# Layer 1's q, k and z projections computed with the weights as the stationary operand

## The chip, the cores and the metric

The kernel runs on one core of one Trainium2 chip. The metric is the device time of one execution in microseconds; of several runs the median is given. Five engines work side by side, each through its own queue in a fixed order: TensorE (PE, with its weight loads shown apart as PEld), VectorE (DVE), ScalarE (ACT), GpSimd (POOL) and SyncE (SP), which issues the transfers.

## What is computed

A decoder trunk of two layers over 256 tokens of width 2048. Layer 0 mixes by a gated spatial unit, layer 1 by causal attention with 16 heads of 128; with 256 tokens there is one key block, so every query sees its own block under the causal mask. Cut to layer 1, which the change touches:

```python
q, k, v, z = split(x @ w_in_b, 4)            # x 256 x 2048, each result 256 x 2048
for h in range(16):                           # heads of 128 columns
    s = q_h @ k_h.T * 128**-0.5               # 256 x 256
    s = where(key <= query, s, -inf)
    o_h = softmax(s) @ v_h
branch = o * silu(z)
y = branch @ w_out
x = layer_norm(ALPHA * x + y)
x = x + sigmoid(x @ w_gate) * (p @ w_proj)
```

All is float32 in, float32 out.

## The kernel before

**Products.** A float32 operand is split by `split` (line 71) or `load_weights` (line 110) into a high part that TensorE's fp32r format holds (a copy on ACT) and the rest (a subtraction on DVE). A product is then three matmuls: high by high, low by high, high by low. An operand's tile of 128 features is kept as `xs[k]`, 128 partitions by [high 256 tokens, low 256 tokens].

**Weights.** They stream through SBUF in chunks of 128 x 2048. `load_weights` fetches a chunk in two halves on SP's queue into `wr` (four buffers), makes `wh` on ACT (L121) and `wl` on DVE (L122); there are three buffers of each, and the loader runs two chunks ahead (`AHEAD`). The list `chunks` (lines 91 to 106) sets their order.

**Row units.** `row_unit` (line 182) takes one chunk: four of the 16 feature tiles, 512 output columns. The 128x128 piece of x is stationary, the 512 columns of weights move. For each k and each half m of the tokens it issues three matmuls of 512 columns, L204, L206 and L208, so 24 in a unit; `row_slice` calls four units for 512 output columns of all 256 tokens, and the result lies token-major in two PSUM banks.

**The order around the units.** At the end of each unit `tick` (line 158) calls what has come due in the list `later`; `at(n, f, ...)` puts a step there for the n-th unit end from now. The final order on each engine is set by the scheduler when the program is built.

**Attention before.** For every 512 columns q and k come by `row_slice` (lines 561 to 569) and are copied to SBUF by ACT (L567). `head` (line 501) turns one head's q and k by four PE transposes of 128x128 (L507, tile `tq`) and splits them; one unit later `scores` (L517 to L522, tile `sc`) forms the three causal 128x128 blocks, DVE and ACT make the probabilities, one unit later `probs` turns the three blocks (L542, tile `pt`) and splits them, and one unit later `values` (L555, tile `ov`) forms the head's output with the probabilities stationary:

```python
for m, bs in ((0, (0,)), (1, (1, 2))):
    steps = [(b, x, y) for b in bs for x, y in ((0, 0), (0, 1), (1, 0))]
    for a, (b, x, y) in enumerate(steps):
        nc.tensor.matmul(ov[:, m], p[:, x, b * P:(b + 1) * P], vk[b // 2][h // 4][:, y, hc], ...
```

That is nine matmuls of 128 columns. `gated` (line 348) then makes z by `row_slice`, multiplies silu(z) into `o` and turns the product by `turn` (L235, four transposes for 256 features) so that it can be the stationary operand of the output projection in `after` (line 381).

Of the kernel before, what the change touches and what calls it, by code (L numbers as in the profile page):

```python
# [10 lines left out]
AF = mybir.ActivationFunctionType  # L11
ALU = mybir.AluOpType

P = 128
D = 2048
S = 256
KT = D // P
NM = S // P
NS = D // 512
# [4 lines left out]
HD = 128  # L24
# [11 lines left out]
def f32(ap):  # L36
    return ap.bitcast(F32)
# [3 lines left out]
def decoder_trunk(ctx: ExitStack, tc: tile.TileContext, xT, pT, wv_a, wu_a, wz_a, w_sT, b_s,  # L41
# [5 lines left out]
    nc = tc.nc  # L47
# [7 lines left out]
    def t2(name):  # L55
        return act.tile([P, 512], F32, name=name, tag="t2", bufs=NT2)

    def t4(name):
        return act.tile([P, 1024], F32R, name=name, tag="t4", bufs=NT4)

    def r4(name):

        return act.tile([P, NM, 512], F32, name=name, tag="r4", bufs=NR4)

    def bank(name):
        return psum.tile([P, 512], F32, name=name, tag="bank", bufs=8)
# [4 lines left out]
    def split(src, n="s", g=2):  # L71

        t = t4(n).rearrange("p (g h s) -> p g h s", g=g, h=2)
        src = src.rearrange("p (g s) -> p g s", g=g)
        nc.scalar.activation(t[:, :, 0, :], src, AF.Copy)
        nc.vector.tensor_sub(t[:, :, 1, :], src, f32(t[:, :, 0, :]))
        return t
# [4 lines left out]
    def by_blocks(w):  # L82

        return [("p (b k c) -> p k b c", dict(b=4, k=4),
                 w[4 * n:4 * n + 4, :, 512 * c:512 * c + 512].rearrange("b p e -> p b e"))
                for n in range(NS) for c in range(4)]

    def flat(src):
        return [("", {}, src.rearrange("p (b e) -> p b e", b=4))]

    chunks = []
# [3 lines left out]
    for i in range(DEPTH):  # L95
        if i == 1:
            for h in range(2):
                for c in range(KT // 2):
                    chunks += flat(wv_b[h, c])
            q, k = by_blocks(wqkz_b[0:KT]), by_blocks(wqkz_b[KT:2 * KT])  # L100
            for n in range(NS):
                chunks += q[4 * n:4 * n + 4] + k[4 * n:4 * n + 4]
            chunks += by_blocks(wqkz_b[2 * KT:3 * KT])
        chunks += by_blocks(w_out[i])
        chunks += flat(w_proj[i, 0]) + flat(w_proj[i, 1])
        chunks += by_blocks(w_gate[i])
# [26 lines left out]
    ident = consts.tile([P, P], F32, name="ident")  # L133
# [20 lines left out]
    def at(units, f, *args):  # L154

        later.append([units, f, args])
# [25 lines left out]
    def row_unit(banks, ks, xs, order=None):  # L182


        NN = len(banks[0])
        pat, kw, wh, wl = weights()
        if pat:
            wh, wl = ([w.rearrange(pat, **kw)[:, i] for i in range(len(ks))] for w in (wh, wl))
            wh, wl = [[w] for w in wh], [[w] for w in wl]
        else:  # L190
            wh, wl = ([[w.rearrange("p (k n c) -> p k n c", k=len(ks), n=NN)[:, i, n] for n in range(NN)]
                       for i in range(len(ks))] for w in (wh, wl))

        def three(i, m, ns):
            k = ks[i]
            c = slice(m * P, (m + 1) * P)
            xh, xl = xs[k][:, 0, c], xs[k][:, 1, c]
            first, last = k == 0, k == KT - 1

            def o(n):  # L200
                return banks[m][n].rearrange("p (b c) -> p b c", b=4) if pat else banks[m][n]

            for n in ns:
                nc.tensor.matmul(o(n), xh, wh[i][n], start=first, stop=False)  # L204
            for n in ns:
                nc.tensor.matmul(o(n), xl, wh[i][n], start=False, stop=False)  # L206
            for n in ns:
                nc.tensor.matmul(o(n), xh, wl[i][n], start=False, stop=last)  # L208

        if order:  # L210
            for m, n in order:
                for i in range(len(ks)):
                    three(i, m, [n])
        else:
            for i in range(len(ks)):
                for m in range(NM):
                    three(i, m, range(NN))
        tick()
# [3 lines left out]
    def row_slice(xs, name="y"):  # L222

        banks = [[bank(name)] for _ in range(NM)]
        for c in range(4):
            row_unit(banks, range(4 * c, 4 * c + 4), xs, both if c == 3 else None)
        return [b[0] for b in banks]

    def turn(xs, j, rows, n="t"):

# [14 lines left out]
    xs = [None] * KT  # L245
# [96 lines left out]
    for n in range(NS):  # L342
        y = row_slice(xs, "u")
# [4 lines left out]
    def gated(o, xs):  # L348

        br = [None] * KT  # L350
        for n in range(NS):
            y = row_slice(xs, "z")
            for m in range(NM):
                t = t2("sz")
                nc.scalar.activation(t, y[m], AF.Silu)
                nc.vector.tensor_mul(o[n][:, m, :], o[n][:, m, :], t)
            for i in range(2):
                at(1 + i, turn, br, 2 * n + i, o, "b")
        return br
# [18 lines left out]
    br = gated(us, xs)  # L378
# [105 lines left out]
    xs = after(0, br)  # L484
# [3 lines left out]
    vk = [[None] * NS for _ in range(NM)]  # L488
# [8 lines left out]
    o = [None] * NS  # L497
    blocks = (slice(0, P), slice(P, 3 * P))
    w3 = slice(0, 3 * P)

    def head(h, q, k):

        c = slice((h % 4) * HD, (h % 4 + 1) * HD)
        tp = bank("tq")
        for j, r in enumerate((q, k)):
            for m in range(NM):
                nc.tensor.transpose(tp[:, j * S + m * P:j * S + (m + 1) * P], r[:, m, c], ident)  # L507
        at(1, scores, h, split(tp, "qk"))

    def scores(h, qk):  # L510
        qh, ql = qk[:, 0, 0, :], qk[:, 0, 1, :]
        kh, kl = qk[:, 1, 0, :], qk[:, 1, 1, :]
        c0, c1 = slice(0, P), slice(P, S)
        sc = bank("sc")

        t = sc.rearrange("p (a b) -> p a b", b=P)[:, 0:4:3, :]
        nc.tensor.matmul(t, qh[:, c0], qk[:, 1, :, c0], start=True, stop=False, skip_group_check=True)  # L517
        nc.tensor.matmul(sc[:, c0], ql[:, c0], kh[:, c0], start=False, stop=True, skip_group_check=True)
        t = sc[:, blocks[1]]
        nc.tensor.matmul(t, qh[:, c1], kh, start=True, stop=False, skip_group_check=True)  # L520
        nc.tensor.matmul(t, qh[:, c1], kl, start=False, stop=False, skip_group_check=True)
        nc.tensor.matmul(t, ql[:, c1], kh, start=False, stop=True, skip_group_check=True)  # L522
        s = t2("sm")
        nc.vector.tensor_add(s[:, w3], sc[:, w3], causal.rearrange("p a b -> p (a b)"))
        nc.vector.tensor_add(s[:, c0], s[:, c0], sc[:, 3 * P:4 * P])
        mx = small.tile([P, NM], F32, name="mx")
        sm = small.tile([P, NM], F32, name="sum")
        for m in range(NM):
            nc.vector.tensor_reduce(mx[:, m:m + 1], s[:, blocks[m]], axis=mybir.AxisListType.X, op=ALU.max)
        nc.vector.tensor_scalar(mx, mx, -QK_SCALE, None, op0=ALU.mult)  # L530
        for m in range(NM):
            nc.scalar.activation(s[:, blocks[m]], s[:, blocks[m]], AF.Exp, scale=QK_SCALE,
                                 bias=mx[:, m:m + 1], accum_out=sm[:, m:m + 1])
        nc.vector.reciprocal(sm, sm)
        for m in range(NM):
            nc.vector.tensor_scalar(s[:, blocks[m]], s[:, blocks[m]], sm[:, m:m + 1], None, op0=ALU.mult)
        at(1, probs, h, s)

    def probs(h, s):
        tp = bank("pt")  # L540
# [6 lines left out]
        at(1, values, h, p)  # L547

    def values(h, p):
        ov = bank("ov").rearrange("p (a c) -> p a c", c=P)  # L550
        hc = slice((h % 4) * HD, (h % 4 + 1) * HD)
        for m, bs in ((0, (0,)), (1, (1, 2))):
            steps = [(b, x, y) for b in bs for x, y in ((0, 0), (0, 1), (1, 0))]
            for a, (b, x, y) in enumerate(steps):
                nc.tensor.matmul(ov[:, m], p[:, x, b * P:(b + 1) * P], vk[b // 2][h // 4][:, y, hc],  # L555
                                 start=a == 0, stop=a == len(steps) - 1, skip_group_check=True)
        if h % 4 == 0:
            o[h // 4] = r4("o")
        nc.scalar.activation(o[h // 4][:, :, hc], ov[:, 0:NM], AF.Copy)

    for n in range(NS):
        rows = []
        for _ in range(2):
            y = row_slice(xs, "qk")
            rows.append(r4("qk"))
            for m in range(NM):
                nc.scalar.activation(rows[-1][:, m, :], y[m], AF.Copy)  # L567
        for h in range(4):
            at(1 + 2 * h, head, 4 * n + h, *rows)

    br = gated(o, xs)
    after(1, br)

# [54 lines left out]
```

## Time and profile before

| what | value |
|---|---|
| median of three runs | 1070.65 us (1070.04 to 1070.73) |
| the profiled execution | 1070.59 us |
| its span in the profile | 1068.9 us |
| mean granted TensorE clock | 0.999 of full speed |
| matmuls on PE | 4944 |
| moved over the span | 203.86 MB, 191 GB/s |

The profiled execution and the median agree to 0.1 us; 1.7 us of the execution lie outside the span. In the profile "busy" is the time in which an engine has at least one instruction under way. Matmuls are pipelined, and their recorded lengths overlap, so what one costs is read from the distance between the starts of two, in the view of instructions in order of time.

### The profile page before, as it was taken

To read this page: it belongs to the slowest core of one execution; us is meant where nothing else is said; L and a number is where in the kernel's file an instruction comes from. 1 tells how busy PE (TensorE), PEld (TensorE's weight loads), DVE (VectorE), ACT (ScalarE), POOL (GpSimd) and SP (SyncE) were. 2 spreads that over 40 slices of the span, in tenths; PEclk is the share of its full clock that TensorE was granted. 3 is DMA by queue.
4 is the path that set the end of the run, shared out by engine and by line. 5 is a ranking of instruction groups with operands and counts; after the bars stand their busy time and mean duration, and the time that the engine had idled before them with its cause. 6 is when DMAs were issued, how large, how long until landed. Compare 5 with 4: busy or idle time off the path is not lost.

```text
span 1068.9 us, 12836 instructions
## 1 busy us (share of the span) xinstructions
PE 1057.5 (99%) x4944; PEld 878.1 (82%) x4944; DVE 616.8 (58%) x763; ACT 499.5 (47%) x659; POOL 24.5 (2%) x46
## 2 busy tenths in 40 slices
PE   8999999999999999999999999999999999999997
PEld 6888888888888878888888888888888888887886
DVE  5646774555555695564545465555566555668552
ACT  5545453545433455444434455454465443345442
POOL 1100110000000000000000000000000000000000
PEclk9999999999999999999999999999999999999999
DMA  7775795566555555555555554444646455555561
GB/s 259 269 257 183 247 299 185 184 204 199 188 184 191 194 169 186 189 182 181 196 197 194 198 160 158 158 158 158 197 158 197 166 199 195 192 184 170 198 204 40
DMA packets 97262, 203.86 MB, mean 191 GB/s; under 512 B 6912, under 2 KB 9232, under 8 KB 97200
## 3 DMA queue, kind: packets, MB, share of 16 engines
q1 hardware_dynamic: 95184, 196.63, 54.9%
q0 software_dynamic: 2016, 6.40, 2.3%
q8 instruction: 39, 0.64, 0.3%
q14 instruction: 23, 0.19, 0.1%
HBM read 200.86 MB, written 2.15 MB: 190 GB/s over the span
## 4 chain that ended last, share of the span: by engine, by line
PE 82%; issue 14%; DMA 2%; DVE 1%; ACT 0%; POOL 0%; SPq 0%; POOLq 0%; ACTq 0%; DVEq 0%
PE qk L204 5%; PE g L208 5%; PE qk L208 5%; PE qk L206 5%; PE g L206 5%; PE g L204 5%; PE y L206 5%; PE y L204 5%; PE y L208 5%; PE z L204 4%; PE z L206 4%; PE z L208 4%; PE u L206 3%; PE u L204 3%; PE u L208 3%
## 5 line engine op out<-in xcount | busy, mean ns | idle before, releaser
L122 DVE TENSOR_TENSOR wl<-wr,wh 128x1024 fp32r<-128x1024 f32 (+1 forms) x366 | 433.4, 1204 | 334.0 <-ACT wh L121 324.7
L121 ACT ACTIVATE wh<-wr 128x1024 fp32r<-128x1024 f32 (+1 forms) x366 | 372.2, 1041 | 466.4 <-PE y L206 152.6
L204 PE MATMUL g<-wh,xn 128*128 128x512 f32 x256 | 101.7, 397 | 0.0
L204 PE MATMUL z<-wh,x 128*128 128x512 f32 x256 | 101.4, 396 | 0.0
L204 PE MATMUL qk<-wh,x 128*128 128x512 f32 x256 | 101.3, 396 | 0.0
L204 PE MATMUL y<-wh,b 128*128 128x512 f32 x256 | 100.1, 391 | 0.0
L208 PE MATMUL g<-wl,xn 128*128 128x512 f32 x256 | 100.0, 391 | 0.0
L208 PE MATMUL qk<-wl,x 128*128 128x512 f32 x256 | 100.0, 391 | 0.0
L208 PE MATMUL z<-wl,x 128*128 128x512 f32 x256 | 100.0, 390 | 0.0
L206 PE MATMUL qk<-wh,x 128*128 128x512 f32 x256 | 99.9, 390 | 0.0
L206 PE MATMUL z<-wh,x 128*128 128x512 f32 x256 | 99.8, 390 | 0.0
L206 PE MATMUL g<-wh,xn 128*128 128x512 f32 x256 | 99.8, 390 | 0.0
L208 PE MATMUL y<-wl,b 128*128 128x512 f32 x256 | 99.7, 389 | 0.0
L206 PE MATMUL y<-wh,b 128*128 128x512 f32 x256 | 99.6, 389 | 0.0
L208 PEld LDWEIGHTS z<-wl,x 128*128 128x128 f32 x256 | 48.1, 188 | 10.2
L208 PEld LDWEIGHTS g<-wl,xn 128*128 128x128 f32 x256 | 48.0, 188 | 10.2
L208 PEld LDWEIGHTS qk<-wl,x 128*128 128x128 f32 x256 | 48.1, 188 | 10.2
L208 PEld LDWEIGHTS y<-wl,b 128*128 128x128 f32 x256 | 48.1, 188 | 10.1
L204 PEld LDWEIGHTS y<-wh,b 128*128 128x128 f32 x256 | 48.1, 188 | 9.9
L206 PEld LDWEIGHTS y<-wh,b 128*128 128x128 f32 x256 | 48.1, 188 | 9.7
L206 PEld LDWEIGHTS g<-wh,xn 128*128 128x128 f32 x256 | 48.2, 188 | 9.5
L206 PEld LDWEIGHTS qk<-wh,x 128*128 128x128 f32 x256 | 48.1, 188 | 9.4
(142 smaller groups left out, 1421.9 us busy)
## 6 DMA issues: line engine op xcount, KB each, us to landing
wr<-in_wqkz_b SPq DMA_DIRECT2D x96, 512.0 KB, 4.1
wr<-in_w_out SPq DMA_DIRECT2D x64, 512.0 KB, 4.1
wr<-in_w_gate SPq DMA_DIRECT2D x64, 512.0 KB, 4.1
wr<-in_wu_a SPq DMA_DIRECT2D x32, 512.0 KB, 4.3
wr<-in_wz_a SPq DMA_DIRECT2D x32, 512.0 KB, 4.1
wr<-in_wv_b SPq DMA_DIRECT2D x32, 512.0 KB, 3.9
wr<-in_wv_a SPq DMA_DIRECT2D x26, 512.0 KB, 5.3
gb<-vecs POOLq DMA_DIRECT2D x24, 256.0 KB, 5.9
```

Of the source, the lines that this page charges most:

```text
L121: nc.scalar.activation(hi[:, c], raw, AF.Copy)
L122: nc.vector.tensor_sub(lo[:, c], raw, f32(hi[:, c]))
L204: nc.tensor.matmul(o(n), xh, wh[i][n], start=first, stop=False)
L206: nc.tensor.matmul(o(n), xl, wh[i][n], start=False, stop=False)
L208: nc.tensor.matmul(o(n), xh, wl[i][n], start=False, stop=last)
```

## The change

q, k and z of layer 1 are made feature-major: `column_unit` takes a chunk that holds one tile of 128 output features for all 16 feature tiles of x. The weight piece is stationary and x moves: one matmul of 512 columns multiplies the high weights by [high x, low x] at once, one of 256 columns multiplies the low weights by high x. The bank then holds two halves of 256 tokens, which `halves_sum` adds (a copy on ACT, an addition on DVE). The values are formed with v stationary and the probabilities moving, so the head's output is feature-major as well; the block of the later queries with the later keys needs one more addition. The transposes of q, k and of the gated branch go. The transposed probabilities are taken two units behind the scores instead of one. The chunks of these weights are fetched in another order and cut, with the same bytes.

```diff
-            q, k = by_blocks(wqkz_b[0:KT]), by_blocks(wqkz_b[KT:2 * KT])
-            for n in range(NS):
-                chunks += q[4 * n:4 * n + 4] + k[4 * n:4 * n + 4]
-            chunks += by_blocks(wqkz_b[2 * KT:3 * KT])
+            for h in range(KT):
+                chunks += flat(wqkz_b[h]) + flat(wqkz_b[KT + h])
+            for f in range(KT):
+                chunks += flat(wqkz_b[2 * KT + f])
...
+    def column_unit(xs, joined=False):
+        ps = bank("f")
+        wh, wl = (t.rearrange("p (k c) -> p k c", k=KT) for t in weights()[2:])
+        for k in range(KT):
+            feature_product(ps, wh[:, k, :], wl[:, k, :], xs, k, joined)
+        tick()
+        return ps
+
+    def feature_product(ps, wh, wl, xs, k, joined=False):
+        lh = (ps[:, 0:S], wl, xs[k][:, 0, :])
...
+            ms = [(ps, wh, xs[k].rearrange("p h s -> p (h s)"))]
+            ms.insert(k < KT - 1, lh)
+        for j, m in enumerate(ms):
+            nc.tensor.matmul(*m, start=k == 0 and j == 0, stop=k == KT - 1 and j == len(ms) - 1,
+                             skip_group_check=True)
+
+    def halves_sum(o, ps):
+        nc.scalar.activation(o, ps[:, 0:S], AF.Copy)
+        nc.vector.tensor_add(o, o, ps[:, S:2 * S])
...
-    def head(h, q, k):
-
-        c = slice((h % 4) * HD, (h % 4 + 1) * HD)
-        tp = bank("tq")
-        for j, r in enumerate((q, k)):
-            for m in range(NM):
-                nc.tensor.transpose(tp[:, j * S + m * P:j * S + (m + 1) * P], r[:, m, c], ident)
-        at(1, scores, h, split(tp, "qk"))
...
-        at(1, probs, h, s)
+        at(2, probs, h, s)
...
     def values(h, p):
...
+        steps = ((0, c0, 0, p[:, 0, c0]), (0, c0, 0, p[:, 1, c0]), (0, c0, 1, p[:, 0, c0]),
+                 (1, slice(P, 3 * P), 0, p[:, :, c1]), (1, slice(P, S), 1, p[:, 0, c1]))
+        for j, (m, n, a, b) in enumerate(steps):
+            nc.tensor.matmul(ov[:, n], vk[m][h // 4][:, a, hc], b, start=j == 0, stop=j == 4,
+                             skip_group_check=True)
...
+        nc.scalar.activation(t, ov[:, 0:S], AF.Copy)
+        nc.vector.tensor_add(t[:, P:S], t[:, P:S], ov[:, S:3 * P])
+
+    def head(h, t):
+        at(1, scores, h, split(t, "qk"))
...
+    for h in range(KT):
+        t = t2("qk")
+        for j in range(2):
+            halves_sum(t[:, j * S:(j + 1) * S], column_unit(xs))
+        head(h, t)
+
+    br = [None] * KT
+    for j in range(KT // 2):
+        t = t2("sz")
+        for u in range(2):
+            halves_sum(t[:, u * S:(u + 1) * S], column_unit(xs))
+        nc.scalar.activation(t, t, AF.Silu)
+        nc.vector.tensor_mul(t, t, o[j // 2][:, j % 2, :])
+        t = split(t, "b")
+        br[2 * j:2 * j + 2] = [t[:, u] for u in range(2)]
     after(1, br)
```

The change moves instructions, so their order on two engines follows, before and changed, over one head of the attention in its steady state. In the rows `x_3143` to `x_3673` are the eight pairs of x's feature tiles, `f` is the bank of a column unit, and a count behind a row stands for instructions alike in a row.

TensorE before: the end of a unit with the scores of one head and the values of the head before, and the start of the next unit.

```order
L208 MATMUL qk<-wl,x_3673 128x512
L517 MATMUL sc<-qk 128x2x128
L518 MATMUL sc<-qk 128x128
L520 MATMUL sc<-qk 128x256
L521 MATMUL sc<-qk 128x256
L522 MATMUL sc<-qk 128x256
L555 MATMUL ov<-vk,pb 128x128 x9
L204 MATMUL qk<-wh,x_3143 128x512
L206 MATMUL qk<-wh,x_3143 128x512
```

TensorE before, one unit later: the four transposes of the next head's q and k stand next to those of the probabilities.

```order
L208 MATMUL qk<-wl,x_3185 128x512
L507 MATMUL tq<-ident,qk 128x128 x4
L542 MATMUL pt<-ident,sm 128x128 x3
L204 MATMUL qk<-wh,x_3305 128x512
```

TensorE with the change: the end of a k unit, with the values of the head before.

```order
L247 MATMUL f<-x_3673,wh 128x512
L247 MATMUL f<-x_3673,wl 128x256 x2
L247 MATMUL f<-x_3673,wh 128x512
L573 MATMUL ov<-pb,vk 128x256 x4
L573 MATMUL ov<-pb,vk 128x128
L247 MATMUL f<-x_3143,wh 128x512
L247 MATMUL f<-x_3143,wl 128x256
L247 MATMUL f<-x_3143,wh 128x512
L247 MATMUL f<-x_3143,wl 128x256
```

The units alternate between 512 and 256 columns, the last two feature tiles with the two short ones side by side; the values are five matmuls. At the end of the q unit stand the three transposes of the probabilities and then the five matmuls of the scores, and no transposes of q and k:

```order
L247 MATMUL f<-x_3673,wh 128x512
L558 MATMUL pt<-ident,sm 128x128 x3
L533 MATMUL sc<-qk 128x2x128
L534 MATMUL sc<-qk 128x128
L536 MATMUL sc<-qk 128x256
L537 MATMUL sc<-qk 128x256
L538 MATMUL sc<-qk 128x256
L247 MATMUL f<-x_3143,wh 128x512
```

VectorE before, from one head's reciprocal of the sums to the next head's masked scores.

```order
L534 RECIPROCAL sum<-sum 128x2
L536 TENSOR_SCALAR sm<-sm,sum 128x128
L536 TENSOR_SCALAR sm<-sm,sum 128x256
L122 TENSOR_TENSOR wl<-wr,wh 128x1024
L76 TENSOR_TENSOR qk<-tq,qk 128x2x256
L546 TENSOR_TENSOR pb<-pt,pb 128x384
L122 TENSOR_TENSOR wl<-wr,wh 128x1024
L524 TENSOR_TENSOR sm<-sc,causal 128x384
L122 TENSOR_TENSOR wl<-wr,wh 128x1024
L525 TENSOR_TENSOR sm<-sm,sc 128x128
```

VectorE with the change, the same stretch.

```order
L550 RECIPROCAL sum<-sum 128x2
L552 TENSOR_SCALAR sm<-sm,sum 128x128
L552 TENSOR_SCALAR sm<-sm,sum 128x256
L252 TENSOR_TENSOR qk<-qk,f 128x256
L122 TENSOR_TENSOR wl<-wr,wh 128x1024
L579 TENSOR_TENSOR o<-o,ov 128x128
L76 TENSOR_TENSOR qk<-qk 128x2x256
L122 TENSOR_TENSOR wl<-wr,wh 128x1024 x2
L562 TENSOR_TENSOR pb<-pt,pb 128x384
L540 TENSOR_TENSOR sm<-sc,causal 128x384
L252 TENSOR_TENSOR qk<-qk,f 128x256
L541 TENSOR_TENSOR sm<-sm,sc 128x128
```

The additions of the halves (L252) stand in the queue, each behind the end of its unit on TensorE, and three of a head's four weight subtractions (L122) stand behind the second of them.

## Rows read from the trace of the kernel before

**Rows 1.** The page's busy times: us, share of the span, instructions.

```profile
PE 1057.5 (99%) x4944; PEld 878.1 (82%) x4944; DVE 616.8 (58%) x763; ACT 499.5 (47%) x659; POOL 24.5 (2%) x46
```

**Rows 2.** The page's chain that ended last, shares of the span by engine.

```profile
PE 82%; issue 14%; DMA 2%; DVE 1%; ACT 0%; POOL 0%; SPq 0%; POOLq 0%; ACTq 0%; DVEq 0%
```

**Rows 3.** Waits of PE: us in total, times, longest us.

```profile
PE pt L542 <- DVE sm L536: 0.5, 1, 0.5
```

**Rows 4.** Order of time, PE: first and last of an undisturbed run of 512-column matmuls (start us, length us).

```profile
589.67 0.39 PE L206 MATMUL qk<-wh,x 128*128 128x512 f32 x1
...
613.01 0.39 PE L208 MATMUL qk<-wl,x 128*128 128x512 f32 x1
```

**Rows 5.** Order of time, PE: turning one head's q and k.

```profile
613.25 0.60 PE L507 MATMUL tq<-ident,qk 128*128 128x128 f32 x4
613.60 0.48 PE L204 MATMUL qk<-wh,x 128*128 128x512 f32 x1
613.91 0.40 PE L206 MATMUL qk<-wh,x 128*128 128x512 f32 x1
```

**Rows 6.** Groups of instructions on PE by line, over the span: busy us, mean ns.

```profile
L507 PE MATMUL tq<-ident,qk 128*128 128x128 f32 x64 | 9.6, 272 | 0.0
...
L235 PE MATMUL tp<-ident,o 128*128 128x128 f32 x32 | 4.8, 272 | 0.0
```

**Rows 7.** Order of time, PE: one head's scores and another's values.

```profile
644.80 0.28 PE L517 MATMUL sc<-qk 128*128 128x256 f32 x1
644.91 0.22 PE L518 MATMUL sc<-qk 128*128 128x128 f32 x1
644.97 0.34 PE L520 MATMUL sc<-qk 128*128 128x256 f32 x1
645.14 0.28 PE L521 MATMUL sc<-qk 128*128 128x256 f32 x1
645.26 0.28 PE L522 MATMUL sc<-qk 128*128 128x256 f32 x1
645.38 1.11 PE L555 MATMUL ov<-vk,pb 128*128 128x128 f32 x9
...
646.62 0.40 PE L206 MATMUL qk<-wh,x 128*128 128x512 f32 x1
```

**Rows 8.** Order of time, PE: layer 0's spatial product, 256 columns each, and what follows.

```profile
134.32 0.88 PE L329 MATMUL sp<-vs,ws 128*128 128x256 f32 x6
135.03 0.40 PE L204 MATMUL u<-wh,x 128*128 128x512 f32 x1
...
135.50 0.39 PE L208 MATMUL u<-wl,x 128*128 128x512 f32 x1
...
136.19 0.39 PE L208 MATMUL u<-wl,x 128*128 128x512 f32 x1
```

**Rows 9.** Groups on PEld by line: busy us, mean ns.

```profile
L208 PEld LDWEIGHTS qk<-wl,x 128*128 128x128 f32 x256 | 48.1, 188 | 10.2
...
L329 PEld LDWEIGHTS sp<-vs,ws 128*128 128x128 f32 x48 | 6.8, 190 | 0.6
```

**Rows 10.** Busy times by stretch: four heads' rounds; us, then each engine's busy us and instructions.

```profile
631.49:684.72 53.23, 53.23 (x277) 45.25 (x276) 31.23 (x56) 26.61 (x48) 0.00 (x0) 1.00 0.49 161
```

**Rows 11.** Groups on DVE by line and shape: busy us, mean ns.

```profile
L76 DVE TENSOR_TENSOR qk<-tq,qk 128x512 fp32r<-128x512 f32 x16 | 10.9, 684 | 1.1 <-ACT qk L75 1.1
...
L76 DVE TENSOR_TENSOR x<-xr,x 128x512 fp32r<-128x512 f32 x7 | 5.2, 752 | 5.8 <-ACT x L75 5.8
...
L525 DVE TENSOR_TENSOR sm<-sm,sc 128x128 f32<-128x128 f32 x16 | 4.5, 282 | 0.1
...
L459 DVE TENSOR_TENSOR sg<-sg,pp 128x256 f32<-128x256 f32 x4 | 1.5, 422 | 12.8 <-ACT sg L458 12.8
```

**Rows 12.** The page's transfers by line: KB each, us to landing.

```profile
wr<-in_wqkz_b SPq DMA_DIRECT2D x96, 512.0 KB, 4.1
...
wr<-in_wv_b SPq DMA_DIRECT2D x32, 512.0 KB, 3.9
```

More of the change, by code (lines that the diff above doesn't have):

```diff
@@ L227, in row_slice @@
         return [b[0] for b in banks]
+    def column_unit(xs, joined=False):
[7 more added lines that the diff above has]
+        lh = (ps[:, 0:S], wl, xs[k][:, 0, :])
+        if joined:
+            ms = [(ps[:, 0:S], wh, xs[k][:, h, :]) for h in range(2)] + [lh]
+        else:
+            ms = [(ps, wh, xs[k].rearrange("p h s -> p (h s)"))]
[6 more added lines that the diff above has]
+        nc.vector.tensor_add(o, o, ps[:, S:2 * S])
     def turn(xs, j, rows, n="t"):
@@ L549, in values @@
     def values(h, p):
-        ov = bank("ov").rearrange("p (a c) -> p a c", c=P)
+        ov = bank("ov")
         hc = slice((h % 4) * HD, (h % 4 + 1) * HD)
[L552 to L556, printed above, removed]
+        c0, c1 = slice(0, S), slice(2 * P, 3 * P)
+        steps = ((0, c0, 0, p[:, 0, c0]), (0, c0, 0, p[:, 1, c0]), (0, c0, 1, p[:, 0, c0]),
[3 more added lines that the diff above has]
+                             skip_group_check=True)
         if h % 4 == 0:
             o[h // 4] = r4("o")
[L559 to L571, printed above, removed]
+        t = o[h // 4][:, (h % 4) // 2, (h % 2) * S:(h % 2 + 1) * S]
+        nc.scalar.activation(t, ov[:, 0:S], AF.Copy)
[16 more added lines that the diff above has]
+        br[2 * j:2 * j + 2] = [t[:, u] for u in range(2)]
     after(1, br)
```

## The prediction

> **What bounds the kernel now.** I read the page's busy times first [rows 1]: PE is busy for 1057.5 of 1068.9 us and no other compute engine for more than 58%. The chain that ended last is 82% PE and 14% unexplained issue time [rows 2]; DVE and ACT hold 1% of it. PE's own waits in the stage that changes come to 0.5 us, once, for a head's probabilities [rows 3]. So the end is set by how long PE needs to start one matmul after another, and a matmul's price is the distance between starts, not its recorded length (0.39 us, which overlaps its neighbour). In an undisturbed stretch 103 matmuls of 512 columns separate the starts at 589.67 and 613.01 [rows 4], 0.2266 us each. Short matmuls come in bursts between them, and every one of them delays the end, because PE has nothing to wait for that could swallow it.
>
> **What goes.**
>
> *Transposes of q and k, and of the gated branch.* From the first of four transposes to the second matmul behind them 0.66 us pass [rows 5]; one matmul of 512 would take 0.227, so a burst of four costs 0.433 us. There are 64 transposes of q and k and 32 of the branch [rows 6], 24 bursts: 24 x 0.433 = 10.4 us.
>
> *Values.* Nine matmuls of 128 columns and the long one behind them take 645.38 to 646.62, 1.24 us [rows 7]; less 0.227 that is 1.013 us a head. In their place come four of 256 and one of 128 columns. With 0.123 us for 256 columns (below) and 0.11 for the one of 128 (it and the 256 behind it span 644.91 to 645.14, 0.23, of which 0.12 belong to the latter [rows 7]) that is 0.60. Saved: 0.41 x 16 heads = 6.6 us.
>
> *The one wait for probabilities.* They are now due two units behind the scores, not one; the 0.5 us [rows 3] goes. What is late next there is the split of q and k, treated below.
>
> Together 10.4 + 6.6 + 0.5 = 17.5 us.
>
> **What is added on PE.** For one tile of 128 output features and one feature tile of x the old form spends six matmuls of 512 on four such tiles, 6 x 0.2266 / 4 = 0.340 us. The new form spends one of 512 and one of 256 columns. There are 48 x 16 = 768 such pairs, so a nanosecond on the pair is 0.77 us. No row shows 512 and 256 in turns; the nearest rows bound the pair:
>
> - Cheapest: the first 256-column matmul behind a long one takes 644.80 to 644.91, 0.11 us [rows 7]. The pair is then 0.337, and the units become 2.3 us shorter.
> - Nearest to it are 256-column matmuls that each have their own weights, as here. In a row they start 0.12 apart (645.14, 645.26, 645.38 [rows 7]; six in 0.71 us [rows 8]). But the long ones behind such a burst are slow for a while. From the first of six (134.32) to the end of five long ones (136.19) pass 1.87 us; less 5 x 0.2266 that is 0.74, or 0.123 us for each short one with its consequences [rows 8]. The pair is 0.350, and 768 of them cost 0.0097 x 768 = 7.5 us more than before.
> - Dearest: every long one is as slow as the two that follow a burst at once, 135.03 to 135.50, 0.235 each [rows 8]. The pair is 0.355 and the units cost 11.6 us more.
>
> I take the middle, 7.5, since it is the only one that holds the after-effect and spreads it over the short matmuls that caused it. By the Trainium skill, "TensorE: Matmul & The Clock Gate", section "Back-to-back issue gap", a gap is the columns over 2.4 plus 2.5 ns, that is 215.8 ns for 512 and 109.2 ns for 256; the pair would then cost 325.0 against 323.7 ns for the old share, an estimate of 1.0 us in all, and the sum would come to 1054.1. The trace shows 226.6 where that rule has 215.8, so I don't use it.
>
> **What is added beside PE, costed at nothing.** Four heads' rounds last 53.23 us with DVE busy for 31.23 [rows 10], 7.8 of 13.3 us a head. Added on DVE per head are two additions of 256 columns (0.42 each), one of 128 (0.28), and a split that reads SBUF instead of PSUM (0.752 against 0.684) [rows 11]: 1.2 us, so 9.0 us in a round that shrinks to about 12.7 (32 pairs of 0.350, 1.5 for scores, probabilities and values). ACT, busy for 26.61 of the 53.23 [rows 10], trades its copies of q and k for copies of half banks. The cover is PE: a weight chunk is split two units before it is used, and the split of q and k has the whole next unit (5.6 us) for two copies and two DVE steps. Should that cover go, PE waits for `wl` or for the scores' operands; that is the first rival.
>
> The additions wait for PE in DVE's queue, and three of four weight subtractions of a head stand behind the second. From the end of the q unit to that addition's end I count 7.6 us (its own unit's end at 0.3 + 0.6 + 5.6 = 6.5, the ACT copy and the addition 0.4 each, the hand-overs), then three subtractions, one addition and the split, 4.7 us: 12.3 of a round of 12.7. The chunk so finished is needed a unit later, so some 5 us remain.
>
> Transfers: the same bytes in 96 issues at the same place in SP's queue; the flat cut that they now have lands in 3.9 us where the old one took 4.1 [rows 12]. POOL's queue keeps its order. No price.
>
> **The sum.** 1070.6 (the profiled execution; the median of the runs is 0.1 higher) - 17.5 + 7.5 = **1060.6 us**. With the ends of the pair's price, 1050.8 and 1064.7.
>
> **Rivals.**
>
> *DVE's queue becomes the bound (slower).* Place: the additions of the halves, L252, in the rounds of the 16 heads. Each waits for PE's unit to end and for ACT's copy, with weight subtractions queued behind. It decides once DVE's busy 9.0 us and its in-order waits exceed the 12.7 us of a round, so with over 3.7 us of waits a head. From there every microsecond costs 16. With 4.8 us of waits it is 1.1 x 16 = 17.6 us on top: 1078. For it: DVE waits for ACT and PE several times in a round, and new waits come in. Against it: in the old rounds it had 5.5 us free of 13.3 and PE never waited for it but once [rows 3, 10]; loads run two chunks ahead. Chance 0.06.
>
> *Weight loads become the bound (slower).* The number of loads in these units rises from 1152 to 1536, and each is recorded at 188 ns [rows 9]. If a matmul could not start before the recorded end of its load, the pair would cost 2 x 0.188 = 0.376 and the units 27.6 us more: 1080.7. Against it: the spatial product's loads are recorded at 190 ns, each with its own matmul, and the matmuls start 0.12 apart all the same [rows 8, 9], so loads overlap. Chance 0.03. The Trainium skill, "Perfetto Trace Analysis", section "Identifying the Most-Contended Engine", judges TensorE by the busy share of its weight loads and not by matmul time; by that rule this is the resource that the change spends more of, and no row here shows long and short matmuls in turns.
>
> *The short matmul hides (faster still).* If each 256 costs 0.11 in the alternation and leaves no slow matmul behind it, the time is 1051 to 1054. For it is the first matmul of a burst; against it the after-effect. Chance 0.05.
>
> *In between.* A smaller wait in the attention's rounds, about 0.5 us a head, takes back 8 us: 1066 to 1072. Chance 0.05.
>
> **How the numbers follow.** The forecast has 0.81. Its range reaches from a pair of 0.341 to one of 0.355, with 1 us of small changes at the top: 1054 to 1066; outside lie the last case, the cheap one and the two slower ones. A measurement of this kernel tells 0.2%, 2.1 us, from no change. Faster by more: 0.81 + 0.05 + 0.02 = 0.88; within it, 0.03; slower, 0.09.
>
> **What would show it right or wrong.** Right: PE without a wait between the value projection and the output projection; in the column units starts 0.23 and 0.12 us apart; still two bursts a head, without the four transposes; the stage from the first q unit to the output projection 10 us shorter; all else as before. The pair's price is the step most likely to be off: the distance of two L247 matmuls of 512 columns, 0.350, gives it directly. A row "PE f <- DVE wl" or "PE sc <- DVE qk" among the waits would show the first rival; distances near 0.376 with PEld without gaps the second. A change in the time of layer 0, which is built the same, would make the comparison itself doubtful.

## The result and the profile after

The changed kernel takes 1058.1 us (median of four runs, 1057.6 to 1058.2) against 1070.7 of the kernel before on the same chip: a ratio of 0.988, 95% interval 0.987 to 0.990. Forecast were 1060.6 us, 10 us less than before; it is 12.6 us less. The profiled execution's span is 1056.3 us, before 1068.9.

The page's busy times, chain by engine and transfers of the changed kernel answer to [rows 1, 2, 12].

```profile
PE 1044.7 (99%) x5168; PEld 879.4 (83%) x5168; DVE 636.2 (60%) x827; ACT 499.0 (47%) x687; POOL 24.2 (2%) x46
...
issue 67%; PE 27%; DVE 3%; DMA 1%; ACT 1%; POOL 0%; SPq 0%; POOLq 0%; ACTq 0%; DVEq 0%
...
wr<-in_wqkz_b SPq DMA_DIRECT2D x96, 512.0 KB, 3.6
```

PE is still busy for 99% of the span. The chain now calls most of its time "issue", where it said PE before. That is no idle time, as the stretch from the first q unit to the output projection shows; why the view follows the chain another way is not known. The stretch is given for the kernel before first, then for the changed one (us; busy us of PE, PEld, DVE, ACT, POOL; clock).

```profile
564.28:868.12 303.84, 303.35 (x1513) 255.40 (x1512) 171.80 (x271) 153.86 (x245) 4.31 (x8) 1.00 0.53 173
```

```profile
564.43:856.49 292.06, 292.06 (x1745) 257.35 (x1744) 191.58 (x335) 153.21 (x272) 0.00 (x0) 1.00 0.52 174
```

This stage is 11.78 us shorter, PE is busy for all of it at the full clock, and DVE does 20 us more work in it. The output projection behind it, in which two of the gated branch's bursts of transposes stood, went from 88.0 to 87.05 us. Together that is 12.7 us. Every other stage from the end of layer 0's first projection on has kept its length to 0.1 us. That first projection varies from one execution to the next, so small differences between kernels are read below from the stage and not from the total.

One head's round in the changed kernel, TensorE in order of time (start us, length us): the values behind a k unit, and the probabilities and scores behind the next q unit.

```profile
650.09 0.69 PE L573 MATMUL ov<-pb,vk 128*128 128x256 f32 x5
650.62 0.45 PE L247 MATMUL f<-x,wh 128*128 128x512 f32 x1
650.91 0.28 PE L247 MATMUL f<-x,wl 128*128 128x256 f32 x1
651.02 0.40 PE L247 MATMUL f<-x,wh 128*128 128x512 f32 x1
651.26 0.28 PE L247 MATMUL f<-x,wl 128*128 128x256 f32 x1
...
655.18 0.40 PE L247 MATMUL f<-x,wh 128*128 128x512 f32 x1
...
656.23 0.49 PE L558 MATMUL pt<-ident,sm 128*128 128x128 f32 x3
656.47 0.37 PE L533 MATMUL sc<-qk 128*128 128x256 f32 x1
```

From 651.02 to 655.18 lie twelve pairs, 0.347 us each. The units of z, which have no bursts between them, are dearer: from one place in a unit to the same place two units on pass 11.30 us, 5.65 a unit and 0.353 a pair.

```profile
838.83 0.40 PE L247 MATMUL f<-x,wh 128*128 128x512 f32 x1
...
850.13 0.40 PE L247 MATMUL f<-x,wh 128*128 128x512 f32 x1
```

PE's recorded waits in the changed kernel are those at the start of the program and around the layer norms and the output; none lies in the column units, nor do those of its weight loads, and the one of [rows 3] is gone.

### The profile page after: what moved, and what is told of

The parts are those of the page before. It is cut to its first block, busy times and chain, and to the rows that moved or that the text cites. A ratio compares the mean times of both kernels' runs of the same rounds, so it can differ in the third digit from the quotient of the medians.

```text
span 1056.3 us, 13379 instructions
## 1 busy us (share of the span) xinstructions
PE 1044.7 (99%) x5168; PEld 879.4 (83%) x5168; DVE 636.2 (60%) x827; ACT 499.0 (47%) x687; POOL 24.2 (2%) x46
## 4 chain that ended last, share of the span: by engine, by line
issue 67%; PE 27%; DVE 3%; DMA 1%; ACT 1%; POOL 0%; SPq 0%; POOLq 0%; ACTq 0%; DVEq 0%
PE g L206 6%; PE g L208 6%; PE g L204 6%; PE v L206 2%; PE v L208 2%; PE v L204 2%; DVE wl L122 1%; PE tp L260 1%; DMA wr<-in_wv_a 1%; PE u L206 1%; PE u L204 1%; PE u L208 0%; DVE v L329 0%; DMA xr<-in_xT 0%; DVE vs L341 0%
## 5 line engine op out<-in xcount | busy, mean ns | idle before, releaser
L122 DVE TENSOR_TENSOR wl<-wr,wh 128x1024 fp32r<-128x1024 f32 (+1 forms) x366 | 433.5, 1204 | 304.4 <-ACT wh L121 292.9
L247 PE MATMUL f<-x,wh 128*128 128x512 f32 x768 | 271.0, 396 | 0.0
L247 PE MATMUL f<-x,wl 128*128 128x256 f32 x768 | 206.2, 279 | 0.0
L247 PEld LDWEIGHTS f<-x,wh 128*128 128x128 f32 x768 | 143.2, 188 | 29.9
L247 PEld LDWEIGHTS f<-x,wl 128*128 128x128 f32 x768 | 144.5, 188 | 2.9
L206 PEld LDWEIGHTS g<-wh,xn 128*128 128x128 f32 x256 | 48.1, 188 | 9.5
L204 PEld LDWEIGHTS g<-wh,xn 128*128 128x128 f32 x256 | 48.1, 188 | 9.3
L204 PE MATMUL z<-wh,x 128*128 128x512 f32 x128 | 50.7, 396 | 0.0
L208 PE MATMUL z<-wl,x 128*128 128x512 f32 x128 | 50.0, 390 | 0.0
L204 PE MATMUL u<-wh,x 128*128 128x512 f32 x128 | 50.0, 390 | 0.0
L206 PE MATMUL z<-wh,x 128*128 128x512 f32 x128 | 49.9, 390 | 0.0
```

The source lines that it names most:

```text
L122: nc.vector.tensor_sub(lo[:, c], raw, f32(hi[:, c]))
L247: nc.tensor.matmul(*m, start=k == 0 and j == 0, stop=k == KT - 1 and j == len(ms) - 1, skip_group_check=True)
```

## The experiments

In all of them "the stage" is that from the first q unit to the output projection: 303.8 us before, 292.1 with the change.

### The two halves of the change

`qk_alone` takes q and k by column units and leaves values, z and its transposes as before.

```diff
-    def values(h, p):        # feature-major
+    def values(h, p):        # as before, nine matmuls
...
-    for j in range(KT // 2): # z by column units
...
+    br = gated(o, xs)
```

> q and k by column units, z, its transposes and the values as before. Theory (PE's starts set the end): 16 bursts of four transposes at 0.433 us and the 0.5 us wait go, 7.4 us; 512 pairs at 0.347 instead of 0.340 us come, 3.6 us; so 3.8 us off the 1070.7 of before: 1066.9 us. Rival (the gain of the change is all in the transposes, the pairs cost what the old matmuls cost): 1063.3 us. Rival (the values and z carry all of the gain): 1070 us or more.

Measured: 1065.0 us (ratio 0.9945, 0.993 to 0.996), the stage 298.8 us, 5.0 less than before where 3.8 were expected. One round of a head lasts 13.02 us, as the first matmul of two scores in a row shows (TensorE in order of time):

```profile
709.16 0.37 PE L532 MATMUL sc<-qk 128*128 128x256 f32 x1
...
722.18 0.37 PE L532 MATMUL sc<-qk 128*128 128x256 f32 x1
```

In the full change a round lasts 12.61 (643.86 to 656.47, the start of L533 above and that of the head before it in the same view). The two kernels' rounds differ only by the values: 0.41 us a head, 6.6 us for 16, which is the forecast's term to the digit.

`values_z_alone` is the other half: q and k by row units with their transposes, values and z in the new form, the probabilities one unit behind the scores as before.

> q and k by row units with their transposes as before, values and z in the new form. Theory: values save 0.47 us a head, 7.5 us, the eight bursts of transposes of the gated branch 3.5 us, 256 pairs at 0.353 instead of 0.340 us cost 3.4 us: 7.6 us off, 1063.1 us, and the two halves of the change add up to it. Rival (a part works only beside the other): the two gains together miss the whole 12.6 us by over 2 us.

Measured: 1064.4 us (0.9945, 0.993 to 0.996); the stage 299.4 and the output projection 87.05, 5.4 us less than before, not 7.6. The two halves together miss the whole by 2.4 us, as the rival said. PE's waits show a place (us in total, times, longest):

```profile
PE pt L568 <- DVE sm L562: 2.3, 4, 1.2
```

`values_z_late_probs` puts the second unit of delay into it.

```diff
-        at(1, probs, h, s)
+        at(2, probs, h, s)
```

> values_z_alone with the probabilities turned two units behind the scores. There the stage from the first q unit to the output projection came out 2.3 us longer than the sum of the parts, and PE waited 2.3 us, four times, for probabilities. Theory (that wait is all that the two halves of the change have in common): the waits go, the span falls by 2 us to 1060.5, 1062.3 us. Rival (the missing time lies in the pairs or the bursts): 1064.4 us as before, within 0.5.

Measured: 1062.1 us (0.992, 0.990 to 0.994), the stage 295.2. The wait is gone; the stage fell by 4.3 us, nearly twice what had been recorded as waiting. The total fell by only 2.3, because the first projection of layer 0, which is the same code, took 1.9 us longer in this execution.

### What the delay of the probabilities is worth

`probs_one_unit` is the full change with `at(1, probs, h, s)` put back.

> The changed kernel with the probabilities turned one unit behind the scores, as before, and not two. In the changed kernel's trace a head's probabilities are ready 1.1 us after the end of the k unit behind which their transposes would now stand. Theory A (the second unit of delay is needed): PE waits about 1 us a head, 16 us, 1074 us, and a wait of the transposes for DVE's normalisation is PE's longest. Theory B (the softmax then runs earlier in DVE's queue, since the split of the previous head's probabilities no longer stands ahead of it): under 0.3 us a head, 1058 to 1063 us.

Measured: 1065.5 us (0.996, 0.994 to 0.997), the stage 299.8, 7.8 us longer than with the delay: 0.5 us a head, between the two theories. PE's waits hold a third of it,

```profile
PE pt L558 <- DVE sm L552: 2.6, 12, 0.3
```

and TensorE's order of time says why:

```profile
651.74 0.40 PE L247 MATMUL f<-x,wh 128*128 128x512 f32 x1
652.34 0.33 PE L558 MATMUL pt<-ident,sm 128*128 128x128 f32 x1 [0.20 <-DVE sm L552]
652.42 0.48 PE L247 MATMUL f<-x,wh 128*128 128x512 f32 x1
652.74 0.38 PE L558 MATMUL pt<-ident,sm 128*128 128x128 f32 x2
```

The transpose starts 0.60 us behind the long matmul where 0.23 is the rule: 0.37 lost, of which 0.20 stand as idle, because the long one's recorded 0.40 us reach into the gap. Read in this way, the starts of the 16 heads' transposes slip by 5.4 us together. The other 2.4 us are not taken apart; the burst now stands in two pieces, and its cost in that form was not measured by itself.

`delay_alone` gives that second unit to the kernel before and nothing else.

> The kernel before with nothing but the probabilities turned two units behind the scores. The prediction counted 0.5 us for this. Theory A (a late probability costs more than the recorded wait, because the start of the transposes slips by more than PE's idle time and their burst then stands apart): the parts of the change add up, with q and k alone -5.0 us and values and z alone -9.6 us in the stage, both of them with this delay in it, and the whole -12.75; so the delay by itself is -1.9 us, 1068.8 us, the stage from the first q unit 301.9 us long against 303.8. Theory B (it is worth the recorded wait): -0.5 us, 1070.2 us.

Measured: 1069.2 us (0.9990, 0.9981 to 0.9999), the stage 303.0: 0.9 us, between the two theories again. The kernel before shows where most of it was (TensorE in order of time):

```profile
825.79 0.39 PE L208 MATMUL z<-wl,x 128*128 128x512 f32 x1
826.65 0.61 PE L542 MATMUL pt<-ident,sm 128*128 128x128 f32 x3 [0.47 <-DVE sm L536]
```

The transposes start 0.86 us behind the long matmul where 0.23 is the rule: 0.63 lost, of which 0.47 stand as the wait. The rounds themselves became no shorter: four of them took 53.23 us before [rows 10], 13.31 each; with the delay a round is 13.32, as the rows below show.

Additivity holds less well than theory A had it. The delay gives 0.9; `qk_alone` gives 4.1 more (5.0 less 0.9), and `values_z_late_probs` 8.8 more (9.63 in the stage and the output projection, less 0.87). That is 13.8 us, where the whole has 12.7. Part of the difference is to be seen in `values_z_late_probs`: there eleven of z's 16 units still have heads' bursts between them, in the full change four, and units between bursts are the cheaper ones. Seven units of 16 pairs at 0.006 us make 0.7 of the 1.1 us, by estimate; the rest is open.

From this kernel to `qk_alone` only q and k change. Two of its scores, three rounds apart (TensorE in order of time):

```profile
643.51 0.37 PE L517 MATMUL sc<-qk 128*128 128x256 f32 x1
...
683.47 0.37 PE L517 MATMUL sc<-qk 128*128 128x256 f32 x1
```

A round is 13.32 us, in `qk_alone` 13.02. The 32 pairs of a round cost 32 x 0.007 = 0.22 us more there, so four transposes of q and k were worth 0.30 + 0.22 = 0.52 us, not 0.433. Two other readings give 0.48. One is the stage: it is 4.1 us shorter in `qk_alone`, and its 512 pairs cost 3.6 us more, together 7.7 us for 16 bursts. The other is the burst of [rows 5] by itself. By the thirteenth long matmul behind the burst the pace of 0.2266 is back; it starts here:

```profile
616.45 0.39 PE L204 MATMUL qk<-wh,x 128*128 128x512 f32 x1
```

From 613.25 that is 3.20 us; less 12 x 0.2266 for the long ones in between it is 0.48.

### What the pair costs, and why

`grouped` issues a unit's long matmuls first and its short ones behind them.

```diff
-        for k in range(KT):
-            feature_product(ps, wh[:, k, :], wl[:, k, :], xs, k, joined)
+        for k in range(KT):
+            nc.tensor.matmul(ps, wh[:, k, :], xs[k].rearrange("p h s -> p (h s)"), start=k == 0, ...)
+        for k in range(KT):
+            nc.tensor.matmul(ps[:, 0:S], wl[:, k, :], xs[k][:, 0, :], ...)
```

> The changed kernel, but a column unit issues its 16 matmuls of 512 columns first and its 16 of 256 behind them. In the changed kernel the pair costs 0.353 us in z's units and 0.347 in those between attention bursts. Theory A (what makes the pair dearer than 0.227 + 0.12 is the change from short to long): it is paid once a unit, 16 x 0.3466 + 0.03 = 5.58 us a unit against 5.65 in z and 5.55 in the others: 1058 us, with z's units 5.58. Theory B (each short matmul costs 0.123 with its consequences wherever it stands): 5.59 us in all units, 1058.5 us. Theory C (a long burst of short matmuls with their own weights runs into a limit of weight loading or issue): starts over 0.13 us apart late in the burst, 1066 us or more.

Measured: 1057.6 us (0.988, 0.986 to 0.989), the stage 292.15, as with turns. A unit of z in order of time on TensorE:

```profile
837.77 2.08 PE L238 MATMUL f<-x,wl 128*128 128x256 f32 x16
839.69 3.82 PE L235 MATMUL f<-x,wh 128*128 128x512 f32 x16
843.34 0.40 PE L238 MATMUL f<-x,wl 128*128 128x256 f32 x2
```

Sixteen short ones take 1.92 us, 0.12 each, and the sixteen long ones behind them 3.65 where 16 x 0.2266 are 3.63. That is 0.02 to 0.03 us lost behind sixteen short ones, as much as [rows 8] shows behind six. So this loss is paid once a burst and not for each short matmul, as theory A had it; the unit's 5.57 us alone could hardly tell A (5.58) from B (5.59). Nor is it paid at every step from short to long: the attention's turns cost 0.347 us a pair, which is 0.227 + 0.12 with no such loss. Late in the burst the starts stay 0.12 apart, so theory C falls. z's units cost 5.57 us against 5.65 in turns; the attention loses what z gains, with rounds of 12.69 us in place of 12.61.

`z_grouped` uses the groups in the last twelve units of z only.

> The changed kernel with the order of the run grouped (512s first, then 256s) in the last twelve units of z only. There the turns cost 5.653 us a unit and the groups 5.567; between attention bursts it was the other way round. Theory: 12 x 0.086 = 1.0 us off the changed kernel's stage, 291.0 us, and 1057.1 us in all, the fastest of these kernels. Rival (the two orders differ only by what stands around them): no change, 1058.1 us.

Measured: the stage 291.1 us, as expected 1.0 less than with the change. In total 1056.1 us (0.9865, 0.985 to 0.988), the fastest kernel here, though its interval overlaps that of the change and only half of the 2.0 us between the two totals lies in the stage.

`even_turns` drops the swap in a unit's last pair.

```diff
-            ms.insert(k < KT - 1, lh)
+            ms.append(lh)
```

> The changed kernel with 512 and 256 in turns to the end of each unit (there the last pair is swapped, so that two of 256 and, across the unit's end, two of 512 are neighbours). In z's units the turns run in a pattern of three pairs, 0.353 us each, in the attention's in one of two, 0.347. Theory A (the neighbours at the unit's end set the slower pattern): z's units fall to 5.55 us, 1 us off the stage. Theory B (what went before has no bearing, the pattern belongs to units without bursts): z's units stay at 5.65 us. In the attention the burst now stands behind a short matmul, whose weight load it follows at once: 0 to 0.1 us a unit more.

Measured: 1058.8 us (0.990, 0.988 to 0.991), the stage 293.75. z's units stay at 5.65: theory B. In the attention the q units became 0.1 us longer, 6.62 against 6.52 from start to start, at the upper end of what was allowed for.

`joined` uses three matmuls of 256 columns for each feature tile.

```diff
-    def column_unit(xs, joined=False):
+    def column_unit(xs, joined=True):
...
-        nc.vector.tensor_add(o, o, ps[:, S:2 * S])
```

> The changed kernel with three matmuls of 256 columns in place of one of 512 and one of 256, so that the halves are added in PSUM and DVE's addition of halves goes (48 of them). Theory (PE bound, DVE covered): 0.12 us each, 0.36 us per feature tile; 32 x 0.21 us in the attention's units and 16 x 0.11 in z's more: 8.4 us slower than the changed kernel, 1066.5 us. Rival (DVE's additions hold PE up): 48 x 0.42 us less on DVE outweighs it, 1058 us or less.

Measured: 1066.7 us (0.9964, 0.995 to 0.998), the stage 300.3, 8.2 us longer: the sum of PE's starts, and nothing given back by the additions that DVE no longer makes. Ten microseconds of z in it, by stretch (us; busy us of PE, PEld, DVE, ACT, POOL):

```profile
850.00:860.00 10.00, 10.00 (x86) 10.00 (x85) 4.67 (x6) 4.61 (x7) 0.00 (x0) 1.00 0.61 201
```

Here the weight loads are recorded as busy all the time, and still 85 of them fall into 10 us, one every 0.12 us, each recorded at some 0.19. The rival of the weight loads, by which 0.188 us would have to pass for each, is refuted by this run as well.

### How deep DVE's cover is

`dve_3us_more` and `dve_6us_more` add seven and fourteen additions of 128x256 to DVE's work in every round, into a tile that nothing reads.

```diff
         at(1, scores, h, split(t, "qk"))
+        for _ in range(7):
+            nc.vector.tensor_add(more, more, t[:, S:2 * S])
```

> The changed kernel with seven more additions of 128x256 on DVE in every head's round, into a tile that nothing reads: 2.9 us on the 8.6 us that DVE is busy in a round of 12.6. Theory (PE is the cover, DVE's queue decides only beyond 3.7 us a round): no change, 1058 us, PE without waits in the column units. Rival (DVE's in-order waits leave no such room): 16 x 1 us or more, 1074 us.

> The same with fourteen additions, 5.9 us: DVE would be busy for 14.5 us of a round of 12.6. Theory: DVE becomes the bound, 1.9 us a round and its waits on top: 1088 us or more, and PE waits for DVE in every round. Rival (the additional work is taken by another resource, or is not in the queue where it was put): under 1065 us.

Measured: 1057.6 us (0.988, 0.986 to 0.990) and 1061.1 (0.9915, 0.9895 to 0.993), the stages 292.05 and 295.5. Four rounds by stretch (us; busy us of PE, PEld, DVE, ACT, POOL), of the changed kernel, with seven, and with fourteen:

```profile
605.90:656.30 50.40, 50.40 (x310) 44.69 (x309) 34.48 (x68) 26.45 (x52) 0.00 (x0) 1.00 0.51 167
```

```profile
606.00:656.40 50.40, 50.40 (x311) 44.68 (x310) 44.69 (x96) 26.41 (x53) 0.00 (x0) 1.00 0.52 173
```

```profile
605.90:656.30 50.40, 50.40 (x309) 44.66 (x308) 50.19 (x122) 27.24 (x52) 0.00 (x0) 1.00 0.50 164
```

With seven DVE is busy for 44.7 of 50.4 us and the time is the same to the tenth. With fourteen it is full, and from the sixth round on a round lasts 12.94 us in place of 12.61. So DVE's queue can become the bound, but the 1088 us or more expected for it were at least 27 too many. PE's list of waits shows none of it; that of its weight loads does (us in total, times, longest):

```profile
PEld sc L536 <- DVE qk L76: 2.6, 9, 0.3
```

So does the order of time (TensorE and DVE, one round of `dve_6us_more`):

```profile
708.09 0.72 DVE L76 TENSOR_TENSOR qk<-qk 128x512 fp32r<-128x512 f32 x1
...
708.31 0.49 PE L561 MATMUL pt<-ident,sm 128*128 128x128 f32 x3
...
708.86 0.39 PE L536 MATMUL sc<-qk 128*128 128x256 f32 x1
```

The scores start 0.55 us behind the first transpose, right after the split of their q and k ends; in the changed kernel it is 0.24 (656.23 to 656.47). The 0.31 us between the two are nearly all that a round has grown by, and only 0.06 of it stand as idle time of PE in the trace. DVE's idle time in four rounds went from 15.9 us to 5.7 with seven additions and to 0.2 with fourteen; between seven and fourteen nothing was tried. One reason why fourteen cost so little is that an addition in a full queue takes less than its length: one starts at 624.43 and the next instruction at 624.76, 0.33 us against a recorded 0.42.

```profile
624.43 0.42 DVE L587 TENSOR_TENSOR more<-more,qk 128x256 f32<-128x256 f32 x1
624.76 0.17 DVE L549 TENSOR_SCALAR mx<-mx 128x2 f32<-128x2 f32 x1
```

## Why the prediction was right, point by point

**What bounds the kernel.** Right: PE's starts made the end of the changed kernel, and the new work on DVE and ACT cost nothing, as `joined` and `dve_3us_more` show from two sides. PE was held up by DVE where the probabilities came one unit behind the scores (`probs_one_unit`, `values_z_alone`) and with fourteen additions. A round's 12.6 us (forecast 12.7) and DVE's 8.6 us in it (34.48 / 4; forecast 9.0) came out as worked.

**The values, 6.6 us.** Measured 6.6, by rounds of 13.02 and 12.61.

**The transposes, 10.4 us.** The mechanism was right, the size too small. The two bursts of the gated branch that stood in the output projection were worth 0.96 us, 0.48 each, and those of q and k 0.48 to 0.52. So 24 bursts make 11.5 us, or 16 x 0.52 + 8 x 0.48 = 12.2. The forecast stopped its count at the second long matmul behind the burst [rows 5]. The ones behind it are still a little late, as the row at 616.45 shows and as [rows 8] showed for another burst; the forecast charged that to the short matmuls of the pair but not to the transposes.

**The wait for probabilities, 0.5 us.** Measured 0.9 by `delay_alone`. A recorded idle time is shorter than the slip of the starts, since a matmul's recorded length goes on into the gap: 0.47 of 0.63 in the kernel before, 0.20 of 0.37 in `probs_one_unit`. The forecast had itself laid down that a matmul's price is read from starts, and then took this one from the waits. It also did not price what the delay is worth inside the change: without it the change gives 4.8 us (`probs_one_unit`, 1070.3 to 1065.5) and not 12.6.

**The pair, 7.5 us.** 0.347 us in the attention's 32 units and 0.353 in most of z's, near 0.350 on the mean; 512 x 0.007 + 256 x 0.013 = 6.9 us. The number was right and the reason given for it was not, so its closeness is partly luck. 0.123 us "for each short one with its consequences" would make the groups cost 0.350 a pair too, and they cost 5.57 / 16 = 0.348 with the loss paid once. The attention's turns cost 0.347 with no loss, and what makes z's turns dearer was not found. By the isolated gap of the Trainium skill, "TensorE: Matmul & The Clock Gate", section "Back-to-back issue gap", the pair is an estimated 325 ns; the trace has 22 to 28 ns more.

**The sum.** 12.2 + 6.6 + 0.9 - 6.9 = 12.8 us, against 12.7 measured in the two stages; with 11.5 for the transposes it is 12.1, so up to 0.6 us is not placed for certain. The forecast's 10.0 fell short by 1.1 to 1.8 in the transposes, 0.6 in the pairs and 0.4 in the wait.

**The rivals.** DVE's queue did not become the bound; it takes 3 us more a round without effect, and becomes it with 6. Weight loads did not; `joined` has far more of them at 0.12 us each, and in the changed kernel PEld's busy time is 879.4 us against 878.1. The short matmul did not hide: the pair is 0.347 at the least, not 0.337. The smaller wait of half a microsecond a head did not come either; `probs_one_unit` has just that, and it is the second unit of delay that kept it away.

Not settled is why turns run in a pattern of 0.347 behind the attention's bursts and of 0.353 without them. It is not the swapped last pair of a unit (`even_turns`).

## What to carry to other kernels

Where one engine is busy throughout, price each change by the distance between starts on that engine, and count a burst of short matmuls until the long ones behind it are back at their own pace; what was cut off there made the largest miss here. Swapping which operand is stationary is then worth what it spares in transposes and in many short matmuls, less the fixed cost of each additional one. Work moved to an engine with slack was free here up to 11.2 us of a round of 12.6, as long as its results were due late enough; one more unit of delay made them so, and was worth 7.8 us in the new order of work, 0.9 in the old.

## What the runs showed that was not expected

- Behind a burst of 256-column matmuls about five long ones are slow, 0.02 to 0.03 us in all, whether the burst has six or sixteen ([rows 8] and `grouped`).
- PE's recorded waits understated what a late operand costs: in `probs_one_unit` 0.20 of 0.37 us for one slip, and over all heads 2.6 us where the starts slip by 5.4 and the stage grows by 7.8. In `dve_6us_more` scores that start 0.31 us late are in no row of PE's waits. The waits of the weight loads show them, but are no measure either: in `probs_one_unit` they come to 7.1 us, with 0.53 for the slip of 0.37. The starts decide.
- From the first matmul of layer 0's first projection to its end the profiled executions took 89.2 (`qk_alone`) to 91.9 us (`values_z_late_probs`), with the same code there. A difference of 1 us between two kernels can't be read from one total each.
